# Attention units split into three parts inside the projection's half blocks, under a fixed TensorE order, with a block-by-block first norm

## The chip, the cores and the metric

The kernel runs on one core of one Trainium2 chip. The metric is the device time of one execution, in microseconds (us), as the median of three runs. A profiled execution gives a trace beside it; all stretches below are counted from the start of its span. Engines are called PE (TensorE), DVE (VectorE), ACT (ScalarE), POOL (GpSimd) and SP (SyncE, which here only issues DMAs). Each engine works through its own list of instructions in order.

## The reference, cut to what matters

The program is a trunk of two layers over 1024 tokens of width 1024. Layer 0 mixes tokens by attention, layer 1 by a recurrent scan; each has a feed-forward part. Only layer 0's attention is touched here:

```python
h = rms_norm(x, norm_mix[0])
proj = h @ w_in + b_in                        # 1024 x (768 + 192 + 192 + 3*768)
qa, ka, va, qb, kb, vb = split(proj)          # rotary embedding on qa, ka, qb, kb
out_a = banded_attention(qa, ka, va, 127, sinks)   # 12 heads, 3 key heads, window of 128
outs = [dilated_attention(qb[g], kb[g], vb[g], win, dil)   # 3 patterns of 4 heads
        for g, (win, dil) in enumerate(((128, 1), (512, 4), (2048, 16)))]
out_b = sum(softmax(lses)[g] * outs[g])       # merge of the three patterns
x = x + concat(out_a, out_b) @ w_out
```

A band attends in blocks of 128 queries to their own block of 128 keys and the one before it.

## The kernel before, in words

Matrix products of the projection are made from three products of halves (high and low part of each operand): `mm3`, lines 171 to 174, adds `wh·hh`, `wh·hl` and `wl·hh` in PSUM. Weights arrive by DMA on SP's queue into `raw` and are split into `wh` (a cast on ACT) and `wl` (a subtraction on DVE), both on line 153.

The attention stage (`attention`, from line 260) has these parts:

- **Norm.** `norm(q)` normalises four blocks of 128 tokens, transposes them on PE (line 203) and writes the gained, split result into `hx` with ACT (line 207) and DVE (line 208). It is called for each half of the tokens.
- **First values.** `first_values(b)` makes the values of the window heads and of pattern 0 for token block b: 24 matmuls of 448 columns (`mm<-vh,hx`), weights `wv` from four loads.
- **Projection.** 24 pieces of 128 columns (`PROJ`), each in two half blocks of 512 tokens. A half block is 24 matmuls of 512 columns (`mm<-hx,wh` and `mm<-hx,wl`). Its end (`take`) is the rotary embedding for queries and keys: ACT writes `rx` (line 253), DVE shuffles it to `ry` (255), POOL multiplies `ry` by the sine table (256), DVE multiplies (257) and adds (312). For values it is an ACT copy with bias (`vT`, 331) and eight PE transposes `tq`.
- **Units.** `unit` is the attention of one block of 128 queries for four heads: on PE the scores `sc` (line 431); on DVE mask, negated maximum and scale in one instruction per head (435, result `pr`); for window units also the sink (438, 439); on ACT the four exponentials (443); for window units the sum, the reciprocal and a product, half on DVE and half on POOL (446, 447, 450); then on PE the transposes `tr` of `pr` (456), on ACT or DVE the copy `pT` (458), and on PE the product with the values `pv` (463), which DVE copies out (464). There are 24 window units (three groups of 8) and 24 pattern units (three groups of 8).
- **The loop.** It takes a half block at a time and, once enough pieces are projected, calls one unit ahead of it. The emission order is a starting point only: a scheduler at build time sets every engine's list, PE's too. The eight units of pattern 2 follow after the last half block.
- **Towards the output product.** Window results go to DRAM (`oT`) and are loaded again into `oraw` (576), which reuses buffers of `kT` and `vt`. `out_proj` then loads `w_out` and runs 24 matmuls per quarter of k; the merge of the patterns (`pattern_weights`, `merge`) needs the statistics `st` and the results `oB` that the units stored.

DRAM traffic that counts here is on SP's queue, except that pattern 2's `oB` goes out on POOL's queue and its `st` on ACT's.

Of the kernel before, what the change touches and what calls it, by code (L numbers as in the profile page):

```python
# [21 lines left out]
P = 128  # L22
# [5 lines left out]
H = 512  # L28
# [51 lines left out]
def lay_out(inp):  # L80
# [22 lines left out]
    v0 = np.concatenate([np.arange(2688, 2944), np.arange(960, 1152)])  # L103
    o["wv0"] = w[:, v0].reshape(NK, P, NV).transpose(1, 0, 2).reshape(P, NK * NV)
# [17 lines left out]
class Trunk:  # L122
# [137 lines left out]
    def attention(self, hp, mp):  # L260
# [14 lines left out]
        hh, hl = self.h_tiles(hp)  # L275

        def norm(q):
            s = slice(q * H, (q + 1) * H)
            for k, ps in self.transposed(p0, psum, [xblk(4 * q + b) for b in range(4)], 5, "tr"):
                self.gained(hh[k][:, s], hl[k][:, s], ps, self.v("nm0", k))  # L280
# [5 lines left out]
        def project(name, take):  # L286
            i = PROJ.index(name)
            wh, wl = self.load_split(wp, a["win"][i], D, "w", 2)
            yield
            for h in range(2):  # L290
                ps = pm.tile([P, H], F32, name="mm", tag="mm")
                for k in range(NK):
                    w, t = slice(k * P, (k + 1) * P), slice(h * H, (h + 1) * H)
                    self.mm3(ps, wh[:, w], wl[:, w], hh[k][:, t], hl[k][:, t], k == 0, k == NK - 1)
                take(ps, bias[:, i:i + 1], h)
                yield
# [61 lines left out]
        streams = [project(n, takes[n]) for n in PROJ]  # L358

        norm(0)  # L360
        next(streams[0])
        next(streams[1])
        self.rope_tables(p0, kp)
# [28 lines left out]
        next(streams[0])  # L392
        next(streams[1])
        for b in range(4):
            first_values(b)
        norm(1)
        e0.close()
        next(streams[0])
        next(streams[2])
        next(streams[1])  # L400
        for b in range(4, NB):
            first_values(b)
# [6 lines left out]
        def toks(t, order, blk):  # L409
            if order == 0:  # L410
                return t[:, blk * P:(blk + 1) * P]
            if order == 1:
                r, lb = divmod(blk, 2)
                return t[:, r + H * lb:H * (lb + 1):4]
            return t[:, blk::8]

        def unit(q, kT, keys, mask, vs, stat, sink, dst):

# [8 lines left out]
            p = ap.tile([P, 4, 256], F32, name="pr", tag="pr", bufs=3)  # L427
            for pr in range(2):
                for e in range(2):
                    r = slice(e * 64, e * 64 + 64)  # L430
                    nc.tensor.matmul(ss[e][:, pr, :n], q[pr][r], kT[pr][r, keys], start=True, stop=True)  # L431
# [12 lines left out]
            if sink is not None:  # L444
# [3 lines left out]
                for pr, eng in enumerate((nc.vector, nc.gpsimd)):  # L448
                    x = p[:, 2 * pr:2 * pr + 2, :n]
                    eng.tensor_tensor(x, x, rd[:, 2 * pr:2 * pr + 2].unsqueeze(2).broadcast_to([P, 2, n]), MUL)  # L450
            for pr in range(2):
                pt = psum.tile([P, H], F32, name="tr", tag="tr")
                for b in range(nk):
                    for e in range(2):
                        s = (b * 2 + e) * P
                        nc.tensor.transpose(pt[:, s:s + P], p[:, 2 * pr + e, b * P:(b + 1) * P], self.ident)
                pT = ap.tile([P, H], F32, name="pT", tag="pT", bufs=3)
                (nc.vector.tensor_copy if pr else nc.scalar.copy)(pT[:, :nk * 256], pt[:, :nk * 256])
                po = pv.tile([P, P], F32, name="pv", tag="pv")
                for b in range(nk):  # L460
                    for e in range(2):
                        s = (b * 2 + e) * P
                        nc.tensor.matmul(po[e * 64:e * 64 + 64], vs[b][2 * pr + e], pT[:, s:s + P], start=b == 0, stop=b == nk - 1)  # L463
                nc.vector.tensor_copy(dst[pr], po)

        def pattern(g):
            stat = ap.tile([P, 8, 2, 4], F32, name="stat", tag="stat")
            os_ = [ap.tile([P, T], F32, name="ob", tag="ob", bufs=2) for _ in range(2)]
# [44 lines left out]
        for u, _ in todo:  # L513
            next(u)
# [1071 lines left out]
```

## Time and profile before

| | |
|---|---|
| time, median of three runs | 2877.0 us (2871.33 to 2877.9) |
| profiled execution, its own time | 2882.99 us |
| span of the profiled execution | 2881.2 us |
| PE busy in the span | 2685.2 us (93%) |
| DVE, ACT, POOL busy | 1806.1, 1185.0, 1096.9 us |
| mean granted TensorE clock | 0.965 |
| norm, first values, first two pieces | 0 to 101 us |
| loop of half blocks and units | 101 to 488 us |
| rest of the units | 488 to 524 us |
| first matmul of the output product | 534.7 us |

In a row of instructions "start, length, engine, line, operation, output<-inputs, shapes, count" a bracket gives the idle time before it and what ended it. A matmul's length includes its way through the array, so neighbours overlap; the distance between starts is what one costs. A float32 matmul has two records. In a row by stretch, each engine has its busy time and count; PEclk is the granted clock, 1.00 being full.

### The profile page before, as it was taken

Reading aid. Unit: us, or ns where it says so; the run is one execution under the profiler, and the core shown is the slowest. Engines: PE = TensorE matmul, PEld = TensorE weight load, DVE = VectorE, ACT = ScalarE, POOL = GpSimd, SP = SyncE. Lnnn points to the kernel's source line nnn. Section 1 sums busy time; section 2 is a strip of 40 time slices with the busy share of each in tenths; the row PEclk is TensorE's granted clock in tenths of the full one; section 3 lists DMA queues with packets and bytes.
Section 4 is the critical chain, followed back from the end, with each engine's and each line's share of the span. In section 5 each row is a group of like instructions: output and inputs, shape, how many; then the busy total and the mean of one; then the engine's idle time right before and its main releaser. Section 6 shows DMA issues by size and latency. Waiting matters only on the chain.

```text
span 2881.2 us, 38009 instructions
## 1 busy us (share of the span) xinstructions
PE 2685.2 (93%) x13302; PEld 2135.8 (74%) x13302; DVE 1806.1 (63%) x3113; ACT 1185.0 (41%) x2329; POOL 1096.9 (38%) x830
## 2 busy tenths in 40 slices
PE   7999999798999999898799899888898999999998
PEld 6777676577888887776577667777777888887776
DVE  4465656557444437888757898768676544444877
ACT  4243435334333334345644454424434433333334
POOL 1121212136443433554444533325643544431644
PEclk9999999899999999999999899889999999999999
DMA  3111111452222227462446366787743222225654
GB/s 125 42 38 38 45 52 38 160 172 92 81 85 81 81 88 263 149 207 78 166 130 168 104 209 168 196 209 206 212 162 127 88 85 80 84 70 187 211 154 161
DMA packets 301393, 366.66 MB, mean 127 GB/s; under 512 B 100984, under 2 KB 175096, under 8 KB 301200
## 3 DMA queue, kind: packets, MB, share of 16 engines
q1 hardware_dynamic: 296416, 350.55, 39.5%
q10 hardware_dynamic: 4496, 12.62, 1.1%
q8 instruction: 105, 1.72, 0.3%
q0 software_dynamic: 288, 1.05, 0.1%
q14 instruction: 88, 0.72, 0.1%
HBM read 268.46 MB, written 95.68 MB: 126 GB/s over the span
## 4 chain that ended last, share of the span: by engine, by line
PE 69%; DVE 16%; DMA 6%; issue 4%; ACT 2%; POOL 2%; SPq 1%; POOLq 0%; DVEq 0%; ACTq 0%
PE y L716 17%; PE z L716 9%; PE pd L864 8%; PE mm L172 4%; PE x L716 3%; PE mm L173 3%; PE mm L174 3%; PE pg L1279 2%; DVE ws L153 2%; PE sc L431 2%; PE pz L172 2%; PE pz L174 2%; PE pz L173 1%; PE pv L463 1%; DVE as L153 1%
## 5 line engine op out<-in xcount | busy, mean ns | idle before, releaser
L864 PE MATMUL pd<-ws,as 128*128 128x512 f32 x1848 | 433.2, 396 | 22.5 <-DVE ws L153 21.4
L864 PEld LDWEIGHTS pd<-ws,as 128*128 128x128 f32 x1848 | 351.7, 191 | 102.0 <-DVE ws L153 26.5
L716 PE MATMUL y<-t,cw 128*128 128x512 f32 x1584 | 370.2, 389 | 0.0
L716 PEld LDWEIGHTS y<-t,cw 128*128 128x128 f32 x1584 | 297.3, 188 | 62.4
L153 DVE TENSOR_TENSOR cw<-raw,cw 128x512 fp32r<-128x512 f32 x264 | 215.0, 816 | 197.7 <-ACT cw L153 191.5
L153 ACT CAST cw<-raw 128x512 fp32r<-128x512 f32 x264 | 163.6, 621 | 246.3 <-PE z L716 104.6
L153 DVE TENSOR_TENSOR wl<-raw,wh 128x512 fp32r<-128x512 f32 (+1 forms) x146 | 145.7, 1000 | 93.2 <-ACT wh L153 92.1
L153 ACT CAST wh<-raw 128x512 fp32r<-128x512 f32 (+1 forms) x154 | 119.7, 779 | 190.3 <-PE po L174 47.6
L725 POOL TENSOR_TENSOR c<-c 128x512 f32<-128x512 f32 x66 | 111.2, 1684 | 188.2 <-DVE c L732 137.1
L720 ACT COPY sn<-y 128x512 f32<-128x512 f32 x132 | 76.9, 587 | 196.2 <-PE y L716 192.8
L172 PE MATMUL mm<-hx,wh 128*128 128x512 f32 x384 | 156.4, 412 | 0.6 <-ACT hx L207 0.6
L173 PE MATMUL mm<-hx,wh 128*128 128x512 f32 x384 | 155.4, 405 | 0.0
L174 PE MATMUL mm<-hx,wl 128*128 128x512 f32 x384 | 154.0, 402 | 0.0
L716 PE MATMUL z<-b,cw 128*128 128x512 f32 x576 | 143.8, 401 | 6.6 <-DVE tx L662 6.6
L256 POOL TENSOR_TENSOR ry<-ry,S 128x512 f32<-128x512 f32 x40 | 52.5, 1314 | 238.5 <-DVE ry L255 238.5
L716 PEld LDWEIGHTS z<-b,cw 128*128 128x128 f32 x576 | 111.8, 194 | 31.3 <-issue 7.0
L153 ACT CAST as<-raw 128x512 fp32r<-128x512 f32 x110 | 68.3, 621 | 153.6 <-PE pd L864 79.0
L716 PE MATMUL y<-b,cw 128*128 128x512 f32 x528 | 129.0, 394 | 0.0
L716 PE MATMUL z<-t,cw 128*128 128x512 f32 x528 | 123.2, 389 | 0.0
L732 DVE TENSOR_TENSOR c<-z,sn 128x512 f32<-128x512 f32 x92 | 63.4, 689 | 85.6 <-ACT sn L720 75.2
L758 POOL TENSOR_TENSOR raw<-s,raw 128x512 f32<-128x512 f32 x44 | 58.9, 1339 | 151.1 <-DVE cw L153 151.0
L716 PEld LDWEIGHTS y<-b,cw 128*128 128x128 f32 x528 | 98.8, 187 | 22.7
(468 smaller groups left out, 6194.5 us busy)
## 6 DMA issues: line engine op xcount, KB each, us to landing
raw<-act SPq DMA_DIRECT2D x132, 256.0 KB
raw<-in_wd SPq DMA_DIRECT2D x132, 256.0 KB
raw<-in_wg SPq DMA_DIRECT2D x88, 256.0 KB
raw<-in_wu SPq DMA_DIRECT2D x88, 256.0 KB
act<-c SPq DMA_DIRECT2D x88, 256.0 KB
raw<-in_wrk SPq DMA_DIRECT2D x32, 512.0 KB
raw<-in_win SPq DMA_DIRECT2D x24, 512.0 KB
raw<-in_wout SPq DMA_DIRECT2D x32, 256.0 KB
```

Of the source, the lines that this page charges most:

```text
L153: return self.nc.scalar.copy(hi, src), (eng or self.nc.vector).tensor_tensor(lo, src, hi.bitcast(F32), SUB)
L172: seen(mm(ps, lh, rh, start=start, stop=False))
L173: seen(mm(ps, lh, rl, start=False, stop=False))
L174: seen(mm(ps, ll, rh, start=False, stop=stop))
L431: nc.tensor.matmul(ss[e][:, pr, :n], q[pr][r], kT[pr][r, keys], start=True, stop=True)
L716: seen(pe.matmul(ps, w[:, x, s], bs[:, k, y], start=start and k == j == 0, stop=k == 3 and j == 2, skip_group_check=True))
L720: ac.copy(s, ps)
L725: po.tensor_tensor(g, g, u, MUL)
L732: ve.tensor_tensor(c[-1], z, s, ADD)
L758: po.tensor_tensor(a11, s, a11, SUB)
L864: pe(ps[b], s[:, x, t], w[:, y], start=first and i == 0, stop=f == N - 1 and i == 2, skip_group_check=True)
L1279: pe.matmul(ps[:, i], bk[rows, h * 4 + i].rearrange("p x t -> p (x t)"), ar[rows, h * 4 + i].rearrange("p y t -> p (y t)"), start=True, st ...
```

## The change

The norm goes block by block: x block, `normed` with the gain from a broadcast load, eight transposes, two copies-with-split of four transposes each; `first_values(b)` follows each block. The first two pieces of the projection are no longer made between the norms but are the first four steps of the loop. `unit` becomes a generator in three parts (scores and softmax; transposes and their copies, both on ACT; products with the values, both pairs in one PSUM tile and one copy out). The loop makes a half block in three parts (9, 9 and 6 matmuls) and calls parts of units between them. Every matmul of units and projection, and every transpose of units, goes through `seen`, which makes it follow the one recorded before it, so that their order on PE is the order of emission. `pr` has 2 buffers instead of 3, `ob` 1 tile of double width, and `oraw` reuses the weights' buffers (`raw`, `wh`, `wl`).

```diff
+        def norm(b, x):
+            xn = self.normed(p0, x, 3, gain)
+            for j in range(2):
+                ps = psum.tile([P, 4, P], F32, name="tr", tag="tr")
+                for k in range(4):
+                    nc.tensor.transpose(ps[:, k], xn[:, (4 * j + k) * P:(4 * j + k + 1) * P], self.ident)
+                self.split(*(z[:, :, b * P:(b + 1) * P] for z in (hz[j], hz[2 + j])), ps)
...
+        last = []
+        def seen(ins):
+            if last:
+                self.after(ins, last.pop())
+            last.append(ins)
...
+        def project(i, h, seen=lambda ins: None):
+            wh, wl = ws[i]
+            ps = pm.tile([P, H], F32, name="mm", tag="mm")
+            for k in range(NK):
+                self.mm3(ps, wh[:, w], wl[:, w], hh[k][:, t], hl[k][:, t], k == 0, k == NK - 1, seen)
+                if k in (2, 5):
+                    yield
+            takes[PROJ[i]](ps, bias[:, i:i + 1], h)
+            yield
...
+        for b in range(NB):
+            norm(b, xs[b])
...
+            first_values(b)
...
         def unit(q, kT, keys, mask, vs, stat, sink, dst):
...
-                    nc.tensor.matmul(ss[e][:, pr, :n], q[pr][r], kT[pr][r, keys], start=True, stop=True)
+                    seen(nc.tensor.matmul(ss[e][:, pr, :n], q[pr][r], kT[pr][r, keys], start=True, stop=True))
...
+            yield
...
+                        seen(nc.tensor.transpose(pt[:, s:s + P], p[:, 2 * pr + e, b * P:(b + 1) * P], self.ident))
+                pTs.append(ap.tile([P, H], F32, name="pT", tag="pT", bufs=3))
+                nc.scalar.copy(pTs[-1][:, :nk * 256], pt[:, :nk * 256])
+            yield
+            po = pv.tile([P, 2, P], F32, name="pv", tag="pv")
...
-                nc.vector.tensor_copy(dst[pr], po)
+            nc.vector.tensor_copy(dst, po)
...
-        todo = [(u, n) for u, n in ((window(0), 2), (pattern(0), 6), (window(1), 8), (pattern(1), 14), (window(2), 16), (pattern(2), 22))
+        todo = [(u, n) for u, n in ((window(0), 4), (pattern(0), 8), (window(1), 10), (pattern(1), 16), (window(2), 18), (pattern(2), 24))
                 for _ in range(NB)]
-        for at in range(2 * 22):
-            i = 2 + at // 2
-            if at % 2 == 0 and i + 1 < len(streams):
-                next(streams[i + 1])
-            if todo[0][1] <= at // 2:
-                next(todo.pop(0)[0])
-            next(streams[i])
-        for u, _ in todo:
-            next(u)
+        before = None
+        for at in range(2 * len(PROJ)):
+            i = at // 2
+            if at % 2 == 0 and 2 <= i + 1 < len(PROJ):
+                weights(i + 1)
+            mm = project(i, at % 2, seen)
+            here = todo.pop(0)[0] if todo[0][1] <= i else None
+            for part in range(3):
+                if here and part == 0:
+                    next(here)
+                if before and part:
+                    next(before)
+                next(mm)
+            before = here
+        for here, _ in [*todo, (None, 0)]:
+            if here:
+                next(here)
+            for _ in range(2):
+                next(before)
+            before = here
...
-        for p, t, m in ((ap, "kT", 2), (ap, "kT", 2), (kp, "vt", 1)):
-            z = p.tile([P, 4, H], F32, name="oraw", tag=t, bufs=m)
+        for t in ("raw", "wh", "wl"):
+            for _ in range(2):
+                z = wp.tile([P, 2, H], F32, name="oraw", tag=t, bufs=2)
```

The eight entries of a group in `todo` are one and the same generator, `window(j)` or `pattern(g)`, eight times; each `next` runs that generator to its next `yield`.

Where instructions stand now is shown at three places. The first is PE's list inside window group 0. In the kernel before, `sc_1424` and `sc_1425` are the scores of one unit, and `pr_1335` belongs to the unit before it, whose scores `sc_1333` and `sc_1334` stand further up the list; `mm_1475` is a half block of the projection.

```order
L431 MATMUL sc_1424<-kTA_105,q_784 128x256
L431 MATMUL sc_1425<-kTA_105,q_784 128x256
L431 MATMUL sc_1424<-kTA_105,q_784 128x256
L431 MATMUL sc_1425<-kTA_105,q_784 128x256
L463 MATMUL pv_1184<-pT_1182,vtA_106 64x128 x4
L172 MATMUL mm_1475<-hx_99,wh_1239 128x512
L173 MATMUL mm_1475<-hx_101,wh_1239 128x512
L174 MATMUL mm_1475<-hx_99,wl_1238 128x512
L456 MATMUL tr_1358<-cst_60,pr_1335 128x128 x4
```

The transposes that follow a unit's scores there read the unit before: between `sc_1334` and `tr_1358` stand 27 matmuls of the projection. The same group in the changed kernel, where `pr_1260` is made from `sc_1258` and `sc_1259` (line numbers are the changed file's):

```order
L449 MATMUL sc_1258<-kTA_106,q_786 128x256
L449 MATMUL sc_1259<-kTA_106,q_786 128x256
L449 MATMUL sc_1258<-kTA_106,q_786 128x256
L449 MATMUL sc_1259<-kTA_106,q_786 128x256
L173 MATMUL mm_1224<-hx_100,wh_1034 128x512
L174 MATMUL mm_1224<-hx_102,wh_1034 128x512
L175 MATMUL mm_1224<-hx_100,wl_1033 128x512
L173 MATMUL mm_1224<-hx_100,wh_1034 128x512
L174 MATMUL mm_1224<-hx_102,wh_1034 128x512
L175 MATMUL mm_1224<-hx_100,wl_1033 128x512
L476 MATMUL tr_1297<-cst_60,pr_1260 128x128 x4
L476 MATMUL tr_1304<-cst_60,pr_1260 128x128 x4
```

Here the transposes of a unit stand six matmuls of the projection behind the scores of the same unit; after them come 9 matmuls, the unit's `pv`, 9 more and the next unit's scores. Only the first unit of each group has 24 matmuls there.

The second place is ACT's list for the same unit of the changed kernel; `rx_1289` is the rotary step of the half block `mm_1224` whose last six matmuls stand in the list above.

```order
L254 ACTIVATE rx_1289<-mm_1224,bias_104 128x512
L461 ACTIVATE pr_1260,ad_1257<-pr_1260,am2_1269 128x256 x2
L458 ACTIVATE ask_1270<-ask_1270 128x4
L461 ACTIVATE pr_1260,ad_1257<-pr_1260,am2_1269 128x256 x2
L478 COPY pT_1302<-tr_1297 128x512
L478 COPY pT_1309<-tr_1304 128x512
```

The unit's exponentials stand behind the rotary step of that half block; on DVE, in four of this group's units, the half block's rotary addition likewise stands ahead of the reciprocal.

The third place is SP's queue at the end of the attention stage, before (`oraw_4473` is the last load of window results, `om_4592` the result of pattern 2):

```order
L576 DMA oraw_4473<-oT_252 128x512 x4
L166 DMA raw_4545<-in_wout 128x512
L166 DMA raw_4594<-in_wout 128x512
L620 DMA x_4680<-in_x 128x1024
L620 DMA x_4700<-in_x 128x1024
L620 DMA x_4720<-in_x 128x1024
L525 DMA mtmp_4563<-st_254 128x8x24
L561 DMA om_4591<-oB_253 128x512
L538 DMA sel_4574<-in_sel 12x768 x2
L561 DMA om_4591<-oB_253 128x512
L561 DMA om_4592<-oB_253 128x512
```

and in the changed kernel:

```order
L559 DMA mtmp_4463<-st_113 128x8x24
L595 DMA om_4491<-oB_112 128x512
L572 DMA sel_4474<-in_sel 12x768 x2
L595 DMA om_4491<-oB_112 128x512
L595 DMA om_4492<-oB_112 128x512
L595 DMA om_4493<-oB_112 128x512
L595 DMA om_4492<-oB_112 128x512
L167 DMA raw_4445<-in_wout 128x512
L167 DMA raw_4494<-in_wout 128x512
```

The loads of window results are all ahead of this piece now, and the first two loads of `w_out` stand behind the load of pattern 2's first result (the second `om_4492`).

More of the change, by code (lines that the diff above doesn't have):

```diff
@@ L357, in attention @@
                 takes[f"v{g}{pr}"] = values(g, pr)
[L358 to L363, printed above, removed]
+        xs = [xblk(0)]
+        nc.sync.dma_start(gain, a["nm0"].broadcast_to([P, D]))
         oT = self.dp.tile([6, P, T], F32, name="oT")
@@ L390, in first_values @@
             nc.vector.tensor_tensor(vtA[:, b], ps[:, 256:NV], bv[:, 256:], ADD)
-        next(streams[0])
-        next(streams[1])
-        for b in range(4):
+        xs += [xblk(b) for b in range(1, 4)]
+        for b in range(NB):
+            norm(b, xs[b])
+            if b == 0:
+                self.rope_tables(p0, kp)
+            if b + 4 < NB:
+                xs.append(xblk(b + 4))
             first_values(b)
-        norm(1)
+            if b in (4, 6):
+                weights(b // 2 - 2)
         e0.close()
[L398 to L402, printed above, removed]
         av.close()
@@ L472, in pattern @@
                 mask = maskC if g == 2 else maskB[:, P:] if first else maskB
[L473 to L475 removed]
+                yield from unit([qs[g][:, pr, b * P:(b + 1) * P] for pr in range(2)], [kTs[g][:, pr] for pr in range(2)],
+                                slice(kb[0] * P, (b + 1) * P), mask, [[vts[g][:, i, h * 64:(h + 1) * 64] for h in range(4)] for i in kb],
+                                (stat[:, b, 0], stat[:, b, 1]), None, toks(os_, g, b))
                 if b == NB - 1:
                     for pr in range(2):
[L478 removed]
+                        (nc.gpsimd if g == 2 else nc.sync).dma_start(oB[g, pr], os_[:, pr])
                     s8 = stat.rearrange("p b s h -> p b (s h)")
@@ L491, in window @@
                 if b % 4 == 0:
-                    os_ = [ap.tile([P, H], F32, name="oa", tag="ol", bufs=3) for _ in range(2)]
+                    os_ = ap.tile([P, 2, H], F32, name="oa", tag="ol", bufs=2)
                 kb = [0] if b == 0 else [b - 1, b]
-                unit([qw[j][:, pr, b * P:(b + 1) * P] for pr in range(2)], [kTA[:, j]] * 2, slice(kb[0] * P, (b + 1) * P),
-                     maskA[:, P:] if b == 0 else maskA, [[vtA[:, i, j * 64:(j + 1) * 64]] * 4 for i in kb], None,
-                     slice(4 * j, 4 * j + 4), [z[:, b % 4 * P:(b % 4 + 1) * P] for z in os_])
+                yield from unit([qw[j][:, pr, b * P:(b + 1) * P] for pr in range(2)], [kTA[:, j]] * 2, slice(kb[0] * P, (b + 1) * P),
+                                maskA[:, P:] if b == 0 else maskA, [[vtA[:, i, j * 64:(j + 1) * 64]] * 4 for i in kb], None,
+                                slice(4 * j, 4 * j + 4), os_[:, :, b % 4 * P:(b % 4 + 1) * P])
                 if b % 4 == 3:
```

51 lines of the change are left out of this document (20 added, 31 removed).

## Prediction

> **What bounds the kernel now.** I read the busy times by stretch first, then PE's waits and its list in time, then one unit's softmax on DVE, ACT and POOL.
>
> ```profile
> 0.00:40.00 40.00, 22.68 (x93) 16.21 (x94) 23.37 (x49) 25.41 (x39) 8.66 (x17) 1.00 0.65 221
> 40.00:102.00 62.00, 57.89 (x264) 51.06 (x264) 18.09 (x36) 11.88 (x18) 4.01 (x3) 0.92 0.07 21
> ...
> 102.00:488.00 386.00, 381.71 (x2178) 279.41 (x2176) 221.09 (x707) 156.88 (x454) 74.55 (x58) 1.00 0.12 41
> ...
> 488.00:524.00 36.00, 28.37 (x254) 17.64 (x252) 27.90 (x114) 22.17 (x84) 3.40 (x3) 1.00 0.16 53
> 524.00:545.00 21.00, 6.39 (x19) 4.66 (x20) 7.20 (x16) 4.60 (x8) 1.97 (x6) 0.61 0.94 312
> ```
>
> From 102 to 488 us PE is the bound: busy 381.7 of 386 at full clock. Its idle time lies at the start, and in the 21 us behind the last unit. So the middle can only get shorter by fewer or cheaper PE instructions, and any wait that is put into PE's list there is paid in full. What PE instructions cost, by the distance of starts:
>
> ```profile
> 130.66 1.14 PE L431 MATMUL sc<-kTA,q 64*128 64x256 f32 x8
> 131.73 0.51 PE L172 MATMUL mm<-hx,wh 128*128 128x512 f32 x1
> 132.07 0.39 PE L173 MATMUL mm<-hx,wh 128*128 128x512 f32 x1
> 132.30 0.40 PE L174 MATMUL mm<-hx,wl 128*128 128x512 f32 x1
> ...
> 312.19 0.40 PE L174 MATMUL mm<-hx,wl 128*128 128x512 f32 x1
> 312.51 0.66 PE L463 MATMUL pv<-pT,vtA 128*64 128x128 f32 x8
> 313.10 0.50 PE L172 MATMUL mm<-hx,wh 128*128 128x512 f32 x1
> ...
> 314.14 0.60 PE L456 MATMUL tr<-cst,pr 128*128 128x128 f32 x4
> 314.50 0.48 PE L173 MATMUL mm<-hx,wh 128*128 128x512 f32 x1
> ```
>
> Scores of a unit: 1.07 (all in us). A projection matmul 0.235, but 0.34 first behind scores or `pv`, and 0.32 last ahead of them (312.19 to 312.51). Four transposes 0.36. One `pv` group 0.59, of which the entry is 0.15: two groups in one run are about 1.03.
>
> **The body without waits.** PE's list in the changed kernel repeats itself: transposes, 9 matmuls, `pv`, 9 matmuls, next scores, 6 matmuls. That is 24 x 0.235 = 5.64, scores 1.07, eight transposes 0.79, `pv` 1.03, and four changes of kind near 0.1 less what the transposes hide: 8.8. Thirty-two units have two key blocks; eight have one and cost 7.7 by halved `tr`, `pv` and scores. With eight half blocks that carry no unit (45) and 32 transposes of values (3.5) this is 282 + 62 + 45 + 4 = 392. Before, the stretch took 386, and 96 matmuls of the first two pieces (22.6) lay ahead of it: 409. So **-17**: the joined `pv` groups and whole score groups. Bounds -22 to -10.
>
> **The wait that is added.** This is where I part from what the description suggests. The lists above show the transposes of a unit 6 matmuls behind its own scores, for seven of the eight units of each group. PE reaches them 1.07 + 0.34 + 5 x 0.235 = 2.58 after the scores' start. When can they start? The softmax of a window unit, by rows:
>
> ```profile
> 131.82 0.43 DVE L435 CUSTOM_DVE_ANT_0 pr<-sc,masks 128x256 f32<-128x256 f32 x1 [0.67 <-PE sc L431]
> ...
> 184.45 0.42 DVE L435 CUSTOM_DVE_ANT_0 pr<-sc,masks 128x256 f32<-128x256 f32 x1
> 185.83 0.69 DVE L312 TENSOR_TENSOR q<-rx,ry 128x512 f32<-128x512 f32 x1
> ...
> 179.50 0.15 DVE L438 TENSOR_TENSOR am<-am,nsinks 128x4 f32<-128x4 f32 x1
> 179.68 0.69 DVE L312 TENSOR_TENSOR q<-rx,ry 128x512 f32<-128x512 f32 x1
> 181.95 0.16 DVE L446 TENSOR_TENSOR ard<-ad,ask 128x4 f32<-128x4 f32 x1 [1.50 <-ACT ask L440]
> 182.15 0.18 DVE L447 RECIPROCAL ard<-ard 128x4 f32<-128x4 f32 x1
> ```
> ```profile
> 174.78 0.69 ACT L253 ACTIVATE rx<-mm,bias 128x512 f32<-128x512 f32 x1
> ...
> 179.74 0.51 ACT L443 ACTIVATE pr<-pr,am 128x256 f32<-128x256 f32 x1 [4.28 <-DVE am L438]
> ...
> 181.73 0.19 ACT L440 ACTIVATE ask<-ask 128x4 f32<-128x4 f32 x1
> ```
> ```profile
> 177.96 1.29 POOL L256 TENSOR_TENSOR ry<-ry,S 128x512 f32<-128x512 f32 x1 [4.35 <-DVE ry L255]
> 182.50 1.46 POOL L450 TENSOR_TENSOR pr<-pr,ard 128x512 f32<-128x512 f32 x1 [3.25 <-DVE ard L447]
> ```
> ```profile
> L331 ACT ACTIVATE vT<-mm,bias x8: 1135/1169/1193, 268.2 to 454.8; 128x512 f32<-128x512 f32 x8
> ```
>
> Scores' start to first mask 1.16 (130.66 to 131.82); four masks 1.38 (184.45 to 185.83); the minimum with the sink then starts at 2.54. From it to the end of POOL's product 4.46 (179.50 to 183.96): 7.0 in all, with nothing in the way. But on ACT the rotary step of the half block stands ahead of the exponentials, and it needs the six matmuls: it starts near 2.78 and takes 0.62, so exponentials start at 3.4, end with the sink's at 5.6 (2.21, 179.74 to 181.95), and POOL's product runs from 6.15 to 7.6. Where DVE's rotary addition (0.61) stands ahead of the reciprocal it is 8.2; where ACT has `vT` (1.17) instead of the rotary step, 8.15. Mean 8.0. The last four transposes then end at 8.46 instead of 2.58 + 0.79 = 3.37: a wait of **5.1** per unit, 21 units (7 in each of three groups): **+107**. Low bound 7.0, so 4.1 and +86. High bound: a unit of the kernel before,
>
> ```profile
> 173.95 1.14 PE L431 MATMUL sc<-kTA,q 64*128 64x256 f32 x8
> ```
>
> whose POOL product ended at 183.96, 10.0 later: 7.1 and +149. There DVE worked for others in between, which the changed lists do less, so I stay near the low end.
>
> Behind the waiting transposes stand on PE the next half block, the unit's `pv` and the next scores; ACT's, DVE's and POOL's next work waits for just these, so no other engine works ahead to shorten the next wait.
>
> Pattern units have no sink and no product, and ACT does their exponentials ahead of the rotary step:
>
> ```profile
> 509.35 0.29 DVE L435 CUSTOM_DVE_ANT_0 pr<-sc,masks 128x128 f32<-128x128 f32 x1
> ...
> 509.68 0.40 ACT L443 ACTIVATE pr<-pr,stat 128x128 f32<-128x128 f32 x1 [0.43 <-DVE stat L435]
> ```
>
> 1.16, then 0.33, then four exponentials of 0.5 give 3.5; transposes end at 3.95, a wait of 0.6: 14 units, **+8** (0 to 20).
>
> **The clock.** PE then idles some 4.6 us in every 14. The kernel before has a stage with idle times like that:
>
> ```profile
> 1641.00:1655.00 14.00, 10.93 (x41) 8.43 (x40) 13.97 (x16) 9.02 (x16) 9.43 (x6) 0.88 0.20 56
> ```
> ```profile
> 1644.39 0.62 PE L173 MATMUL pv<-wl,xi 128*128 128x512 f32 x1 [3.07 <-DVE wl L153]
> 1644.81 0.63 PE L174 MATMUL pv<-wh,xi 128*128 128x512 f32 x1
> ...
> 1658.10 0.67 PE L173 MATMUL pv<-wl,xi 128*128 128x512 f32 x1 [1.80 <-DVE wl L153]
> ```
>
> Behind 3.07 of idling a matmul costs 0.42 (1644.39 to 1644.81) instead of 0.235 for a while, and the mean clock over 14 us is 0.88: 14 x 0.12 = 1.7 us lost. I take 1.8 per window unit: 21 x 1.8 = **+38**. Bounds 0 and +71 (twice as much, if it stays low for twice as long).
>
> [...]
>
> **Start, tail, end.** Before, the first loop matmul came at 101; less the 22.6 that moved, 79.
>
> ```profile
> 101.05 0.36 PE L174 MATMUL mm<-vh,hx 128*128 128x448 f32 x1
> 101.25 0.39 PE L172 MATMUL mm<-hx,wh 128*128 128x512 f32 x1
> ```
>
> Now: 192 matmuls of 0.205 (39) and 64 transposes (7), from about 13, when the first block and its weights are split, and some 6 for the cold start: 65. So **-14** (-18 to -5). The gain's load (512 KB) and DVE's product with it lie under each block's 4.9 us of matmuls; uncovered they would cost about 1.2 per block.
>
> The tail's pattern units now also run one behind the other on PE: 0.75 to the masks, 0.33, four exponentials 1.56, transposes 0.25, two copies on ACT 0.7, `pv` 0.4 and three handovers 0.4: 4.4 each, 35 for eight, and 2.5 for the last window unit, against 36: **+2** (-6 to +8).
>
> ```profile
> 534.67 0.80 PE L172 MATMUL po<-wh,o 128*128 128x512 f32 x1 [11.15 <-ACT wh L153]
> ...
> 543.65 1.94 PE L551 MATMUL tr<-cst,e 128*44 128x128 f32 x8 [3.93 <-POOL e L548]
> ```
> ```profile
> DMA to landing us min/median/max: 5.2/6.3/7.4
> ```
>
> At the end, 11.15 behind the last unit and 3.93 for the merge. The first is not won: the loads of `w_out` now stand behind pattern 2's result, whose stores take 5.2 to 7.4 to land (second row), and then need 4 to arrive and be split. The merge's statistics are now loaded early, so the 3.93 and some 2 of half clock behind it go: **-6** (-11 to +3).
>
> What I cost at nothing: both `pT` copies on ACT (2 x 0.58, under 9 matmuls of 2.1; without that cover 1.3 per unit); two buffers for `pr` (its last reader stands a whole step earlier); weights one piece ahead (two steps, over 17 us, for 512 KB). The rest of the program keeps its work; its lists differ here and there.
>
> **Sum.** -17 - 14 - 6 + 2 + 107 + 8 + 38 = +118 on the profiled execution's 2883: 3001. That execution was 6 above the median of 2877, so **2995**.
>
> **Rivals.**
> 1. *The clock stays up.* The idle time is broken by the first four transposes, and scores and matmuls fill two thirds of a step. For it: a gap of 1.37 left the clock alone, since the eight matmuls behind it took 0.59 as elsewhere:
>
> ```profile
> 491.22 0.66 PE L463 MATMUL pv<-pT,vtA 128*64 128x128 f32 x8 [1.37 <-DVE oa L464]
> ```
>
> Against it: the rows at 1644 and 1658. Without the term: 2957. [...]
> 2. *The softmax takes as long as before*, 10.0 instead of 8.0, with `wl` subtractions, copies and additions in DVE's way: 21 x 2 = 42 more, 3037. For it: the unit at 173.95; against: DVE's changed list has little between masks and reciprocal.
> 3. *Scores ahead of their use* (faster). If PE had the scores of a unit a full step ahead of its transposes, as the description reads, 24 matmuls and more would cover the softmax, both wait terms and the clock term vanish, and -17 - 14 - 6 + 2 = -35 is left: 2842. It decides where the waits fall under 35 / 35 = 1.0 us per unit, a softmax of under 4.0. Against it: the list itself, and 4.46 from the sink's minimum to POOL's end alone.
>
> **Chances.** Forecast 0.66 (2960 to 3030), rival 1 0.15, rival 2 0.14, rival 3 0.05. About 0.3% (9 us) is what can be told from no change. Only rival 3 is faster, and I leave 0.01 of it for waits that just eat up the gains: faster 0.04, same 0.01, slower 0.95. For the range I take in rival 1's 2957 with its own spread and most of rival 2: 2940 to 3055.
>
> **What would show it.** Right: among PE's waits, `tr` (now line 476) waiting for POOL's `pr` by some 5 us in 21 places; the granted clock under 0.95 between 100 and 600; the loop near 540 instead of 386; first loop matmul near 65; the first `po` still 9 to 12 behind the last `pv`. Wrong: PE busy for over 95% in the loop, or `tr` released by ACT. The forecast falls if PE's transposes hardly wait.

## The result and the profile after

The changed kernel takes 3012.4 us (median of four executions, 3010.1 to 3014.4) beside 2877.5 for the kernel before: 1.047 times as long, 95% interval 1.0455 to 1.0491. The forecast was 2995, with a range of 2940 to 3055. Its profiled execution took 3011.29 us and has a span of 3009.5.

The view by stretch, with the busy time of PE, PEld, DVE, ACT and POOL, then PE's granted clock: start, loop, tail with the wait behind it, output product.

```profile
0.00:62.00 62.00, 48.87 (x245) 42.35 (x246) 33.83 (x64) 25.70 (x42) 8.31 (x15) 1.00 0.46 154
62.00:603.00 541.00, 448.08 (x2357) 330.41 (x2355) 227.29 (x654) 183.10 (x505) 81.31 (x62) 0.90 0.10 33
603.00:666.00 63.00, 32.53 (x186) 20.34 (x185) 24.69 (x105) 27.01 (x101) 5.63 (x8) 0.56 0.25 82
666.00:731.00 65.00, 64.06 (x262) 48.06 (x262) 41.07 (x57) 22.10 (x38) 20.21 (x18) 0.95 0.60 211
```

The loop, in which PE was busy for 382 of 386 us before, now has PE busy for 448 of 541, at a clock of 0.90. What PE waited for between 62 and 603 us (total, times, longest):

```profile
PE tr L476 <- DVE pr L468: 72.3, 16, 5.3
PE tq L356 <- ACT vT L352: 9.1, 5, 2.0
PE tq L356 <- ACT vt L357: 7.1, 4, 1.8
PE tr L476 <- ACT pr L461: 4.0, 9, 0.5
PE tr L476 <- POOL pr L468: 0.4, 2, 0.2
```

One window unit in the list by time shows how such a wait comes about:

```profile
137.64 1.14 PE L449 MATMUL sc<-kTA,q 64*128 64x256 f32 x8
...
139.98 0.40 PE L175 MATMUL mm<-hx,wl 128*128 128x512 f32 x1
140.31 0.16 DVE L456 TENSOR_TENSOR am<-am,nsinks 128x4 f32<-128x4 f32 x1
140.41 0.69 ACT L254 ACTIVATE rx<-mm,bias 128x512 f32<-128x512 f32 x1 [8.06 <-PE mm L175]
141.00 0.50 ACT L461 ACTIVATE pr<-pr,am 128x256 f32<-128x256 f32 x1
...
143.31 0.69 DVE L333 TENSOR_TENSOR kT<-rx,ry 128x512 f32<-128x512 f32 x1
143.91 0.17 DVE L465 RECIPROCAL ard<-ard 128x4 f32<-128x4 f32 x1
144.12 0.69 DVE L468 TENSOR_TENSOR pr<-pr,ard 128x512 f32<-128x512 f32 x1
144.25 1.45 POOL L468 TENSOR_TENSOR pr<-pr,ard 128x512 f32<-128x512 f32 x1 [0.98 <-DVE ard L465]
144.96 1.94 PE L476 MATMUL tr<-cst,pr 128*128 128x128 f32 x8 [4.58 <-DVE pr L468]
146.54 0.78 PE L173 MATMUL mm<-hx,wh 128*128 128x512 f32 x1
147.12 0.63 PE L174 MATMUL mm<-hx,wh 128*128 128x512 f32 x1
147.54 0.63 PE L175 MATMUL mm<-hx,wl 128*128 128x512 f32 x1
```

PE has done its six matmuls by 140.4; the softmax ends at 145.7, 8.07 behind the scores' start; the transposes start when DVE's half of the product is done; and the projection behind them costs 0.42 per matmul instead of 0.235. The rotary step (140.41) stands ahead of the exponentials and the rotary addition (143.31) ahead of the reciprocal.

The end of the stage, in PE's list by time:

```profile
609.40 0.80 PE L449 MATMUL sc<-kT,q 64*128 64x128 f32 x4 [4.96 <-DVE q L333]
...
665.85 0.79 PE L173 MATMUL po<-wh,o 128*128 128x512 f32 x1 [11.53 <-ACT wh L154]
...
671.57 1.35 PE L585 MATMUL tr<-cst,e 128*44 128x128 f32 x8
```

The wait of the output product (`po`) for `w_out` is there as before, 11.5; the merge's wait of 3.93 is gone; a new wait of 5.0 stands in the tail.

To compare kernels I cut PE's loop, from the first to the last projection matmul, into three parts by the distances of starts: idle gaps of over 0.25 us; what matmuls cost above their mean at full clock where the record of the granted clock says half; and the rest. The loop here is 540.7 us (61.9 to 602.6): 405.7 of rest, 97.5 of gaps and 37.5 of half clock. The kernel before has 386.6 (101.2 to 487.9), 4.2 of it gaps and no half clock.

### The profile page after: what moved, and what is told of

The parts are those of the page before. It is cut to its first block, busy times and chain, and to the rows that moved or that the text cites. A ratio compares the mean times of both kernels' runs of the same rounds, so it can differ in the third digit from the quotient of the medians.

```text
span 3009.5 us, 38002 instructions
## 1 busy us (share of the span) xinstructions
PE 2724.7 (91%) x13302; PEld 2163.9 (72%) x13302; DVE 1789.2 (59%) x3017; ACT 1200.3 (40%) x2377; POOL 1106.4 (37%) x830
## 3 DMA queue, kind: packets, MB, share of 16 engines
q0 software_dynamic: 288, 1.05, 0.1%
## 4 chain that ended last, share of the span: by engine, by line
PE 68%; DVE 15%; DMA 6%; issue 4%; ACT 3%; POOL 3%; SPq 1%; POOLq 0%; DVEq 0%; ACTq 0%
PE y L751 16%; PE z L751 8%; PE pd L899 6%; PE mm L173 4%; PE mm L174 3%; PE x L751 3%; PE mm L175 3%; PE tr L476 2%; DMA raw<-in_wd 2%; PE pg L1314 2%; DVE ws L154 2%; PE po L173 2%; PE po L174 2%; PE po L175 2%; PE pz L173 2%
## 5 line engine op out<-in xcount | busy, mean ns | idle before, releaser
L173 PE MATMUL mm<-hx,wh 128*128 128x512 f32 x384 | 175.4, 457 | 0.0
L174 PE MATMUL mm<-hx,wh 128*128 128x512 f32 x384 | 161.7, 421 | 0.0
L175 PE MATMUL mm<-hx,wl 128*128 128x512 f32 x384 | 160.9, 419 | 0.0
L476 PE MATMUL tr<-cst,pr 128*128 128x128 f32 x320 | 69.9, 365 | 87.8 <-DVE pr L468 72.3
L476 PEld LDWEIGHTS tr<-cst,pr 128*128 128x128 f32 x320 | 48.6, 182 | 109.4 <-issue 72.4
L453 DVE CUSTOM_DVE_ANT_0 pr<-sc,masks 128x256 f32<-128x256 f32 (+1 forms) x192 | 61.7, 376 | 98.0 <-PE sc L449 97.9
```

What stands on the lines that cost most here:

```text
L173: seen(mm(ps, lh, rh, start=start, stop=False))
L174: seen(mm(ps, lh, rl, start=False, stop=False))
L175: seen(mm(ps, ll, rh, start=False, stop=stop))
L453: nc.vector.tensor_tensor_reduce(p[:, h, :n], ss[e][:, pr, :n], mask, -0.125, 3e38, ADD, ALU.min, nm[:, h:h + 1])
L476: seen(nc.tensor.transpose(pt[:, s:s + P], p[:, 2 * pr + e, b * P:(b + 1) * P], self.ident))
```

## The experiments

The later stages differ between these kernels although nothing in them was edited: the scheduler's lists there come out a little differently each time, and one kernel's executions differ too (by up to 27 us, in the run with 18 matmuls between). From the first matmul of the next stage's filter (`z<-b`) to the end of the span it takes 2201.5 us in the kernel before, 2203.9 in the changed one, and between 2184.9 and 2217.2 in the twelve others, in one execution of each; how much of this is the lists and how much the execution was not separated. So I judge each experiment in the attention stage by the start of that `z<-b` (before 679.7, changed 805.6), and by its whole time only beyond some 15 us.

### A generator for each unit

```diff
-            for b in range(NB):
+            def one(b):
...
                 yield
+            return [one(b) for b in range(NB)]
...
-        todo = [(u, n) for u, n in ((window(0), 4), ...) for _ in range(NB)]
+        todo = [(u, n) for us, n in ((window(0), 4), ...) for u in us]
```

> The changed kernel, but each unit is a generator of its own, so that a unit's scores stand 33 projection matmuls ahead of its transposes on PE instead of 6. Theory (PE waits for the softmax because the scores are too late, and the half clock follows from these waits): the 97 us of gaps and the 37 us of half clock that the changed kernel's trace has between 62 and 603 us vanish, down to the few us of the kernel before; with the pattern units of the tail no longer one behind the other some 15 more: 3012 - 93 - 35 - 15 = 2869, between 2845 and 2890, so not slower than before. Rival (the given order as such, both copies of pT on ACT or two buffers of pr cost the time): most of the waits stay, over 2940.

Measured: 2879.1 us, 1.0001 times the kernel before (0.9988 to 1.0014); `z<-b` at 667.2. The loop, by stretch, and all that PE waited for in it:

```profile
63.00:464.00 401.00, 398.33 (x2357) 300.63 (x2356) 213.20 (x659) 187.21 (x513) 83.30 (x63) 1.00 0.14 45
PE pv L485 <- ACT pT L478: 2.2, 5, 0.6
```

The same work takes 401 us instead of 541, at full clock, and no transpose waits. The softmaxes got no shorter (6.9 to 9.6 us from the scores to POOL's end); PE just has other work meanwhile. In the attention stage this is 138 us better than the changed kernel and 12.5 better than the kernel before. The total doesn't show the latter, since the later stages took 15.7 longer in the profiled execution. The rival, that the order as such, the copies on ACT or the two buffers of `pr` cost the time, is out for the loop.

### No given order

```diff
         def seen(ins):
-            if last:
-                self.after(ins, last.pop())
-            last.append(ins)
+            return
```

> The changed kernel without the given order: the matmuls are not chained to each other, so the scheduler sets PE's list; the rest, pr with 2 buffers and the copies on ACT too, stays. In its list the transposes stand 19 to 39 matmuls behind their scores in window units (one of 24 units: 6) and 10 to 35 in the first 16 pattern units. Theory (distance sets the wait): waits of the transposes under 15 us in all, clock near 1.00 in the loop, about 2865 (2845 to 2890). Rival (buffers and copies cost the time, not the order): over 2950.

Measured: 2852.3 us, ratio 0.9896 (0.9875 to 0.9917); `z<-b` at 651.2. The loop:

```profile
62.00:465.00 403.00, 403.00 (x2341) 303.06 (x2340) 219.20 (x649) 183.65 (x505) 81.79 (x62) 1.00 0.14 45
```

PE doesn't wait at all in the loop. The rest of the change, taken with the scheduler's own order, makes a kernel that is 1% faster than the one before.

### Transposes 18 matmuls behind their scores

The kernel with a generator per unit, with the parts called in another order:

```diff
-                if here and part == 0:
+                if here and part != 1:
                     next(here)
-                if before and part:
+                if before and part == 1:
                     next(before)
                 next(mm)
...
             if here:
                 next(here)
-            for _ in range(2):
-                next(before)
+            next(before)
+            if here:
+                next(here)
             before = here
```

> As the run with a generator per unit, but the transposes of a unit stand 18 projection matmuls and one group of pv behind its own scores instead of 33. Theory (a wait is the length of the softmax less the distance on PE): PE gets there 1.07 + 2.3 + 1.03 + 2.2 = 6.6 us after the scores' start, a window unit's softmax takes 7.0 to 8.8, so 0.4 to 2.2 of wait, about 1.0, in each of 24 window units and none in pattern units: +24 (10 to 50) against that run in the attention stage, first matmul of the next stage's filter (row z<-b) near 691 instead of 667, total near 2900 (2885 to 2935). Rival (any distance inside one step costs alike, since the half clock sets in at every wait): waits of 2.5 us and more, 2950 or more.

Measured: 2901.2 us, ratio 1.0072 (1.005 to 1.0094); `z<-b` at 684.3. PE's waits in the loop:

```profile
PE tr L476 <- DVE pr L468: 20.7, 16, 1.8
PE tr L476 <- POOL pr L468: 2.7, 15, 0.2
```

23 us of waits, as worked out from the length of the softmax less the distance, and only 3.2 of half clock, though each of 16 units still waits 0.75 to 1.75. So a wait does not cost clock by itself (the last section has a stretch with waits that half clock followed, and one that it did not). That the total came within 2 us of the expected 2900 is luck in part: `z<-b` came 17 us behind that of the run with a generator per unit, not 24, because the loop grew by 32 while the tail, whose order the edit changes too, got 11 shorter and the stretch behind it 4.

### The window units' product left out

```diff
-                for pr, eng in enumerate((nc.vector, nc.gpsimd)):
-                    x = p[:, 2 * pr:2 * pr + 2, :n]
-                    eng.tensor_tensor(x, x, rd[:, 2 * pr:2 * pr + 2].unsqueeze(2).broadcast_to([P, 2, n]), MUL)
```

> The changed kernel with the last product of the window units left out (the probabilities are not scaled by the reciprocal of their sum, so the window results are not normalised); PE's list is the same. Theory (PE waits for the softmax's end): the transposes are then released by the exponentials, some 2 us earlier in 16 units that waited for DVE's product: 3012 - 16 x 2.1 = 2978, and down to 2960 if the shorter gaps cost less clock. Rival (the end of the softmax is not what PE waits for): 3000 or more.

Measured: 2941.3 us, ratio 1.0211 (1.0193 to 1.023): the direction is the theory's, the size twice what I expected. The loop is 477.9 us, with 36.6 of gaps and 21.2 of half clock. One unit's transposes and matmuls:

```profile
140.81 0.33 PE L473 MATMUL tr<-cst,pr 128*128 128x128 f32 x1 [1.27 <-ACT pr L461]
141.30 0.92 PE L473 MATMUL tr<-cst,pr 128*128 128x128 f32 x4 [0.16 <-ACT pr L461]
...
142.94 0.78 PE L173 MATMUL mm<-hx,wh 128*128 128x512 f32 x1
```

A wait of 4.58 became one of 1.27 and two of 0.16 (the second stands ahead of three more transposes at 142.38), 3.0 shorter and not 2.1: the first transpose needs only the first exponential, while the product had to wait for the sum over all four heads.

### Matmuls in the gap

```diff
                 pt = psum.tile([P, H], F32, name="tr", tag="tr")
+                for _ in range(18 if fill and pr == 0 else 0):
+                    seen(nc.tensor.matmul(pt, hh[0][:, 0:P], hl[0][:, 0:H], start=True, stop=True))
```

> The changed kernel with 18 matmuls of 512 columns (4.2 us) that nobody reads put on PE ahead of the transposes in 13 window units, those whose transposes wait 4.4 to 5.3 us. Theory (the wait is set by the softmax, and the half clock behind it is a second cost that comes from the idling): the time gets shorter although work is added: half clock of 13 of 20 waits gone, 3012 - 13 x 1.9 = 2988 (2975 to 2998). Rival 1 (the clock does not hang on the idling, or the half clock costs nothing): 3012 or, with the added work on the path, up to 3012 + 13 x 4.2 = 3066.

Measured: 2988.5 us, where 2988 was expected; ratio 1.0378 (1.0362 to 1.0393). The same unit as above:

```profile
141.41 4.28 PE L474 MATMUL tr<-hx 128*128 128x512 f32 x18
146.21 0.63 PE L478 MATMUL tr<-cst,pr 128*128 128x128 f32 x4 [0.52 <-DVE pr L468]
...
147.43 0.48 PE L173 MATMUL mm<-hx,wh 128*128 128x512 f32 x1
147.75 0.40 PE L174 MATMUL mm<-hx,wh 128*128 128x512 f32 x1
```

234 matmuls more, and 24 us less. The transposes still start when the softmax is done, but the projection behind them runs at 0.235 again: half clock went from 37.5 to 12.8 us, and gaps from 97.5 to 42.7 because the added matmuls fill them. The wait and the clock are two costs.

The loops side by side (in the third row the 234 added matmuls are part of the rest):

| kernel | matmuls between a window unit's scores and its transposes | loop, us | rest | gaps | half clock |
|---|---|---|---|---|---|
| changed | 6 (first of a group 24, eighth of two groups 15) | 540.7 | 405.7 | 97.5 | 37.5 |
| no product | as above | 477.9 | 420.0 | 36.6 | 21.2 |
| matmuls in 13 gaps | as above, and 18 added | 520.1 | 464.6 | 42.7 | 12.8 |
| 18 behind | 18 | 433.1 | 406.8 | 23.2 | 3.2 |
| generator per unit | 33 | 400.9 | 397.9 | 3.0 | 0 |
| no given order | 19 to 39, one 6 (its transposes come in the tail) | 403.1 | 403.1 | 0 | 0 |

### The tail without the given order

The kernel with a generator per unit; `seen` chains nothing behind the last half block.

```diff
-            if last:
+            if last and not tail:
                 self.after(ins, last.pop())
...
+        tail.append(1)
         for here, _ in [*todo, (None, 0)]:
```

> As the run with a generator per unit, but the order on PE is given only up to the last half block of the projection; the eight pattern units behind it are ordered by the scheduler. Theory (in the tail the given order puts each unit's matmuls behind the copies of the unit before it): the tail shrinks from 50 to about 35 us, first z<-b at 652 instead of 667, total 2864, give or take the 15 us by which the lists of the later stages differ between these kernels. Rival (ACT's exponentials and copies set the tail): z<-b stays at 667.

Measured: 2852.9 us, ratio 0.9909 (0.9888 to 0.993); `z<-b` at 656.4, 10.8 earlier than with the order given throughout, of 15 expected. PE's waits behind the last half block, first with the order given, then, up to 517 us, without:

```profile
PE po L173 <- ACT wh L154: 12.5, 1, 12.5
PE pv L485 <- ACT pT L478: 9.4, 8, 2.8
PE sc L449 <- DVE q L333: 8.5, 1, 8.5
```
```profile
PE sc L450 <- DVE q L334: 5.1, 1, 5.1
PE pv L486 <- ACT pT L479: 2.1, 1, 2.1
```

The wait of `po` for `w_out` is there without the order too (12.8, ended at 517.0). Most of the wait of `pv` for its copies goes; ACT's work did not set that part of the tail. Where there is no projection to put between, a fixed order of scores, transposes and products only makes units wait for each other's copies.

### The start alone

The kernel before, with the norm block by block and the first two pieces behind it; units and end as they were.

> The kernel before with one part of the change alone: the norm block by block with the broadcast gain, and the first two pieces behind it. Units, their order and the end stay. Theory (the start is worth what it was worth in the changed kernel): first projection matmul with units at 62 + 23 = 85 instead of 101, z<-b 17 earlier at 663, total 2860 give or take the later lists' 15. Rival (the gain is taken up again by the loop, whose units then lack softmax work done early): z<-b less than 6 earlier.

Measured: 2867.7 us, ratio 0.9953 (0.9936 to 0.997); `z<-b` at 664.5, 15.2 earlier. First projection matmul:

```profile
61.88 0.40 PE L173 MATMUL mm<-hx,wh 128*128 128x512 f32 x1
```

The gain of the changed kernel's start (61.90 there) is the norm's and is kept by the rest of the stage.

### The end: five attempts at one wait

All five start from the kernel without the given order. First, loads on POOL's queue:

```diff
-            nc.sync.dma_start(ms, st.rearrange("(b p) g e -> p b g e", p=P))
+            nc.gpsimd.dma_start(ms, st.rearrange("(b p) g e -> p b g e", p=P))
...
-                    nc.sync.dma_start(l[g], oB[g, pr][:, q * H:(q + 1) * H])
+                    (nc.sync if q else nc.gpsimd).dma_start(l[g], oB[g, pr][:, q * H:(q + 1) * H])
```

> As the run without the given order, but the loads of the statistics and of the first half's pattern results go out on POOL's queue, so that the loads of w_out no longer stand on SP's queue behind loads that wait for stores. Theory (the 12 us of idling ahead of the first po is SP's queue): the first po starts within 2 us of the last pv, z<-b at 638 instead of 651, total 2852 - 13 = 2839 (2825 to 2855). Rival (something else is late too, w_out's buffers or the split of the window results): less than 4 us won, 2848 or more.

Measured: 2847.3 us, ratio 0.9887 (0.9871 to 0.9904); first `po` 2.7 earlier, its wait 7.9 instead of 12.1, `z<-b` at 649.7. By `z<-b` 1.5 us are won, so the rival's bound of 4 us holds; the total is 5.0 less, within what the later stages differ by. Then the table `sel` cleared and loaded at the head of `pattern_weights`:

> As the run with loads on POOL's queue, but the constant table of the merge is cleared and loaded first, since there SP's queue still stood behind that load, which waits for POOL to clear its place behind the load of the statistics. Theory (what is left of the wait ahead of the first po is still SP's queue): the first po starts within 2.5 us of the last pv instead of 7.9, z<-b 6 to 9 earlier than in that run, near 642; total near 2843 (2830 to 2855). Rival (the place of w_out's loads comes free only with the last units): no change, z<-b at 650.

Measured: 2849.1 us, ratio 0.991 (0.9893 to 0.9927); the wait stays at 8.0, `z<-b` at 653.2. The loads of `w_out` went out at 499.1, five us ahead of the last `pv`, and still nothing was won; the rival is right that nothing changes, but not why, since the loads' place was free early. ACT's list shows why:

```profile
503.33 0.37 ACT L478 COPY pT<-tr 128x256 f32<-128x256 f32 x1 [0.93 <-PE tr L476]
511.66 0.28 ACT L568 ACTIVATE ev<-ev 128x96 f32<-128x96 f32 x1 [7.96 <-DVE ev L567]
511.85 1.12 ACT L154 CAST wh<-raw 128x512 fp32r<-128x512 f32 x2
```

The cast of `w_out` stands behind the merge's exponential, which waits for the statistics. In a kernel made from this one, DVE's subtractions for the window results were moved behind the tail's copies, two by two:

```diff
-            nc.vector.tensor_copy(dst, po)
+            outs.append(nc.vector.tensor_copy(dst, po))
...
-                self.split(os2[q][k // 4][:, k % 4, 0], os2[q][k // 4][:, k % 4, 1], raws[6 * q + k])
+                self.after(self.split(os2[q][k // 4][:, k % 4, 0], os2[q][k // 4][:, k % 4, 1], raws[6 * q + k])[1], outs[40 + 3 * q + k // 2])
```

> As that, and DVE's subtractions for the window results stand two by two behind the copies of the last pattern units instead of ahead of the last query's rotary addition. Theory (the 5.7 us that the scores wait for the last q, and part of the wait in the changed kernel's tail, are these subtractions): the wait falls to 2 or less, the first po comes another 3 to 6 earlier, z<-b near 637, total near 2838 (2825 to 2852). Rival (q is late because of the rotary chain through ACT and POOL itself): the wait stays over 4, and the first po does not come earlier.

Measured: 2863.8 us, ratio 0.9953 (0.9938 to 0.9967). The wait of the scores for the last `q` fell from 5.7 to 1.1. Part of it only moved, since PE now waits 2.6 for `pr` just ahead of it. `q` itself is done 6.5 us behind the start of the last projection matmul instead of 9.3: the subtractions were some 2.8 us of its lateness, not all of it. And the first `po` came at 512.3 as before, with a wait of 9.5, and `z<-b` at 651.2: the last `pv` came 1.7 earlier (502.5), and that gain is waited for one step later. Next, the exponential behind the first cast of `w_out` on ACT:

```diff
-            nc.scalar.activation(ev, ev, AF.Exp, scale=-1.0)
+            self.after(nc.scalar.activation(ev, ev, AF.Exp, scale=-1.0), self.splits[0])
```

> As the run with the constant table first, but the exponential of the merge's weights stands behind the cast of the first piece of w_out on ACT. There that exponential stood ahead of the cast and waited 8 us for the statistics, while the piece of w_out had been asked for at 499 us. Theory (three queues in a row held the same wait: SP's, then SP's behind POOL, then ACT's): the first po starts within 2.5 us of the last pv instead of 8, z<-b near 647 instead of 653; total near 2843 (2832 to 2858). Rival (the merge is the bound: its statistics come late, and the time saved ahead of the first po is waited for at the merge): the first po comes early, but z<-b stays within 2 us of 653.

Measured: 2850.9 us, ratio 0.9901 (0.9872 to 0.9929), `z<-b` at 654.5. The first `po` follows the last `pv` at once, and the second waits in its place, for a subtraction that stands behind the merge on DVE. This is the rival's sign, with `z<-b` within 2 us of 653:

```profile
505.80 0.80 PE L173 MATMUL po<-wh,o 128*128 128x512 f32 x1
...
514.00 0.19 DVE L565 TENSOR_TENSOR mtmp<-mtmp 128x32 f32<-128x32 f32 x1 [7.09 <-DMA mtmp<-st]
...
515.37 0.79 PE L174 MATMUL po<-wl,o 128*128 128x512 f32 x1 [8.77 <-DVE wl L154]
```

Last, DVE's first step of the merge behind `w_out`'s subtraction, and the merge's transposes two pieces of `w_out` later on PE:

```diff
-            nc.vector.tensor_tensor(mx, ms[:, :, 0, 0:4], ms[:, :, 1, 0:4], ALU.min)
+            self.after(nc.vector.tensor_tensor(mx, ms[:, :, 0, 0:4], ms[:, :, 1, 0:4], ALU.min), self.splits[1])
...
-                        if merged and k in ((0, 1, 2), (0, 1, 2))[c]:
+                        if merged and k in ((2, 3, 4), (0, 1, 2))[c]:
```

> As the run with the exponential behind the cast, but on DVE too the merge's first step stands behind w_out's subtraction, and on PE the merge's transposes stand behind 36 matmuls of the output product instead of 12. In that run the first po came at 505.8, right behind the last pv, but the second waited 8.8 us for the subtraction, and the merge's e was there only at 520.5. Theory (the merge's statistics are the last thing to come, about 15 us behind the last pv; what PE does meanwhile decides): 36 matmuls cover half of these 15 us, z<-b 6 to 9 earlier than in that run, near 647, total near 2843 (2830 to 2855). Rival (the subtraction waits for something else, or the loads of w_out do not keep up): po waits 5 us or more again, z<-b at 652 or later.

Measured: 2854.1 us, ratio 0.9907 (0.989 to 0.9923), `z<-b` at 658.2: nothing won. PE's waits from 500 to 535 us:

```profile
PE tr L585 <- POOL e L582: 5.8, 1, 5.8
PE po L174 <- DVE wl L154: 1.0, 1, 1.0
```

The product now runs right behind the units, and the merge waits. Here it is the merge that stands behind `w_out`: its last step on DVE (`ev<-ev,mtmp`) follows a subtraction that waited for a cast.

```profile
524.92 0.69 DVE L154 TENSOR_TENSOR wl<-raw,wh 128x512 fp32r<-128x512 f32 x1 [4.36 <-ACT wh L154]
525.53 0.25 DVE L573 TENSOR_TENSOR ev<-ev,mtmp 128x96 f32<-128x96 f32 x1
```

These kernels' tails also got longer (last `pv` at 508.8 here, 499.4 without these edits). All five lie between 649.7 and 658.2 at `z<-b`. Four of the edits took away the wait they aimed at, or part of it (the second freed the loads, not the wait), and PE waited elsewhere instead. What hardly changed is the way to the merge: its first transposes (`tr<-cst,e`) start 17.0 us behind the last `pv` without these edits and 13.4 to 17.9 with them, and `z<-b` follows 131.6 to 135.5 later in all six. Whether those 12 us can be won by more than the edits shown stays open.

## Why the prediction was right, point by point

The terms, in us, against the traces (the two pieces that moved into the loop, 22.6, are counted with the loop before: 409.2):

| term | predicted | measured | from |
|---|---|---|---|
| start | -14 | -17 | 101.2 - 22.6 = 78.6 becomes 61.9 by the first loop matmul |
| body without waits | -17 | +1 | rest of the loop 382.4 + 22.6 becomes 405.7 |
| waits in the loop | +107 and +8 | +93 | gaps 4.2 become 97.5 |
| half clock | +38 | +37.5 | |
| tail | +2 | +16 | last loop matmul to last `pv`: 35.4 becomes 51.3 |
| wait for `w_out`, end | -6 | -5 | last `pv` to `z<-b`: 156.4 becomes 151.7 |
| later stages | 0 | +2 | `z<-b` to the end |

In sum +118 was forecast for the profiled execution, and +128 came (+135 between the medians). That is partly luck: the body and the tail came out some 32 above their terms and the waits 22 below theirs, and these misses nearly cancel. Body and tail are both outside the bounds given for them (-22 to -10 and -6 to +8).

**The start** was 3 better than forecast. I took some 6 us for slow first matmuls, which no run shows; the first nine of the first values took 4.0 (starts at 12.71 to 16.73), where nine at 0.205 take 1.8, so about 2.

**The wait.** Right in place and cause: distance on PE against length of the softmax. Its size came out a fifth smaller. The softmax, worked out as 8.0 from rows of the kernel before, took 8.07 and about 8.7 in turn in the first group. The first four transposes wait only for DVE's half of the product, so the waits name DVE and not POOL as I had written (16 against 2), and the 13 longest are 4.4 to 5.3. In five units the wait fell wholly or partly on the value transposes `tq` instead. The count of units was wrong too, in the sum and above it where only the first unit of a group is excepted: six of a group have 6 matmuls between, not seven. In the first two groups the eighth has 15, because its transposes come only after the next group's first scores; these two waited 3.05 each. In the third group the eighth unit's transposes come in the tail. So the loop has 18 such units, not 21. Rival 3, scores ahead of their use, is what the kernel with a generator per unit makes of the description: the attention stage gets shorter than before, by 12.5 where the sum for that case had 35. Rival 2, the softmax as long as before, did not come.

**The clock.** 37.5 against 38: the trace has 20 periods of half clock in the loop, some 1.9 us lost in each, where I had 21 of 1.8. Rival 1, the clock stays up, did not come: all 13 waits of `tr` of 4.4 us or more were followed by matmuls at half clock, 0.42 to 0.43 from start to start. With bounds of 0 and 71 and one row of another stage as the source, so near a hit is luck, but the cost is real: the kernel with added matmuls, where 37.5 became 12.8, shows it as a cost of its own. The kernel before has the same at 1658.10, where 1.80 of idling were followed by matmuls at 0.42.

**The body** is one term that was mis-sized. With waits gone (generator per unit) the rest is 397.9, so the saving is 7 and not 17: a step costs about 9.0 where I had 8.8. The other 8 of the changed kernel's rest (405.7) are in part waits of under 0.25 us: 36 transposes at full clock follow each other by over 0.12 us where 0.11 is usual, about 3 us in all. What the other 5 are stays open.

**The tail** is the other. I had 4.4 per pattern unit; the scores' starts are 4.9 apart. What I left out is the clock: from 603 to 654 it was 0.58, where the kernel before had 1.00 in its tail, and a `pv` group takes 1.05 there (627.78 to 628.83) where I had 0.4.

```profile
627.78 1.12 PE L485 MATMUL pv<-pT,vt 128*64 128x128 f32 x8
628.83 1.23 PE L449 MATMUL sc<-kT,q 64*128 64x128 f32 x8
...
633.73 1.23 PE L449 MATMUL sc<-kT,q 64*128 64x128 f32 x8
```

And the early loads of the window results, which I booked as a gain at the end, brought their subtractions into DVE's list ahead of the last rotary addition: the wait of 5.0 for `q`. The run that moved these subtractions, in a kernel without the given order, shows them to be some 2.8 us of it there.

**The wait for `w_out`** had the forecast's size, but the named cause, SP's queue, was only the first of four lists in which something stood behind the merge.

**What I cost at nothing** held in the loop: both copies on ACT and two buffers of `pr` are in the kernel without the given order too, where PE waits for nothing. The start's gain is confirmed alone.

## What to carry to other kernels

When an order is fixed by hand, count for each producer how much work stands between it and its consumer, and compare with the length of the chain between them; here a loop with 6 matmuls between them took 140 us longer than the same loop with 33, and eight entries of one generator were enough to turn the one into the other. A wait on a busy TensorE can cost twice, as here: 97.5 us in gaps, and 37.5 us of half clock behind them. And before moving a wait out of one engine's list, look in which other lists the same late value has work queued behind it.

## What the runs showed of the hardware

In the loop of the changed kernel the granted clock is recorded as 1.00 or 0.50, and every period of one value lasts a multiple of 3.41 us: 7 of the 20 periods of half clock last 3.41, the other 13 last 6.83. Rows by stretch of that length, of the kernel without the product:

```profile
138.91:142.33 3.42, 1.84 (x8) 0.78 (x6) 2.33 (x9) 2.75 (x11) 1.15 (x1) 1.00 0.00 0
142.33:145.74 3.41, 3.36 (x10) 2.78 (x11) 0.90 (x3) 1.05 (x2) 0.12 (x1) 0.50 0.02 7
```

and of the kernel with 18 matmuls between:

```profile
123.70:127.11 3.41, 1.87 (x10) 1.08 (x8) 1.03 (x3) 1.46 (x8) 1.48 (x1) 1.00 0.00 0
127.11:130.53 3.42, 3.38 (x19) 2.43 (x20) 0.45 (x1) 2.60 (x4) 0.00 (x0) 1.00 0.00 0
```

PE busy for 1.84 of 3.42 us was followed by half clock, 1.87 of 3.41 by full. The traces of the changed kernel and of the kernel before have, from 62 to 600 us, 271 such stretches at full clock: in the 248 followed by full clock PE was idle for at most 0.47 of the stretch, in the 23 followed by half clock for at least 0.58. The first row above, 0.46 idle with half clock behind it, lies on the other side, so these stretches give no sharp limit. Nor does the length of one wait tell: that row holds a wait of 1.27 and shorter ones behind it (the unit shown with that kernel), while in the kernel with 18 matmuls between, 16 waits of 0.75 to 1.75 came with only 3.2 us of half clock in all.
